# One diffusion-transformer step on one core: q and gate tiles evicted by ScalarE, a modulation piece's rows multiplied in reverse, the first rotary copy emitted earlier

## The chip, the cores and the metric

The kernel runs on one core of one Trainium2 chip. A core has TensorE (PE in the profile, with its weight loads as PEld), VectorE (DVE), ScalarE (ACT), GpSimd (POOL) and SyncE (SP), whose queue issues nearly all DMAs here. Each engine runs its instructions in the order of its own queue; semaphores join the queues. The metric is the device time of one execution in microseconds (us), as the median of several runs.

## What is computed

The reference is one step of a two-layer diffusion trunk on 640 tokens (128 context, 512 latent) with 2048 channels, all in float32. Cut to what matters here:

```python
m = silu(cond) @ w_mod + b_mod                 # modulation: shift, scale, gate (6144 columns), for two conditions
h = rmsnorm(x, g) * (1 + scale) + shift
# layer 0: latent attention (A, 8 heads) beside a bidirectional recurrence (B, "HGRN", 8 heads)
q_lat, kv_lat, k_pe, a_gate, b_q, b_ff, b_fb, b_i, b_gate = split_cols(h @ w_in, AB_SIZES)
q = rmsnorm(rmsnorm(q_lat, ..) @ w_q_up, ..)   # the last 64 of 192 channels of a head get a rotary embedding
o_a = blocked_attention(q, keys, vals) * silu(a_gate)
qb = silu(b_q);  o_b = hgrn_bidir(qb, b_i, b_ff, b_fb, ..)
o_b = rmsnorm(o_b) * silu(b_gate)
x = x + gate * (concat([o_a, o_b]) @ w_out)
# layer 1: windowed grouped-query attention, with its own modulation, input and output projection
```

## The kernel before

The tokens lie on the free axis: a tile of 128 channels is 128x640, and a matmul's result holds 128x320 of it, so each tile of a projection is two halves (HALF = 320) in two PSUM banks of the tag `acc`. There are two such banks in the stages below, so the first half of a tile must be evicted before the next tile may begin.

Products of full precision are made of three matmuls on float32 values split in a high and a low part (`three`, L113 to L115): high weight by high activation, high by low, low by high. The third (L115) is the one that needs the low part of the weights. `unit` brings 512 KB of weights (the DMA at L100, into one of four `raw` buffers), and `split` makes the two parts: L75 on ScalarE copies the high part, L76 on VectorE subtracts. `coltile` runs one tile of the projection from the normalised input: two units, each 48 matmuls (8 blocks by three, for each of the two halves).

The stages, with their times in the profile before: start, modulation and first part of the input projection (0 to 245 us); the eight HGRN heads (245 to 980), about 92 us each; the gates of attention heads 2 to 7 and what the latent attention sets up (980 to 1050); the latent (MLA) attention heads, into which the first half of the output projection is woven (`out_b`, to about 1370); the other half; the second layer (from 1500).

**An HGRN head** (`hgrn_head`) runs coltile for the two forget gates, for q, for v (`vr`) and, later, for its output gate. `evict_silu` (L496 on) takes q and the output gate out of PSUM: two VectorE operations of 128x320 (L501, a copy bounded below by XMIN), a sigmoid of three ScalarE operations (`sigmoid`, L70 to L72), one product. `attn_gate` uses it for the attention's gates too (tile `lat`). Beside this stand the recurrence's scans (L539, L540) and its pieces on VectorE, ScalarE (L554, L603) and TensorE (L578, L604).

**Modulation beside the heads.** `pump`, called once a unit, takes the next piece of one of two streams. One is `mod_sums`, on VectorE: loads at L310, sums at L317, four small matmuls at L323. The other is `mod_blocks`, on TensorE: pieces of two weight rows, each row a 512 KB load (L290) into a `raw` buffer and four matmuls of 128x256 (L292) that are summed in the bank `m` over all 16 rows. The `raw` buffers are shared by `unit`, both streams and `head_prep`.

**The start of the MLA heads** (in `run`). Eight finished mix tiles are loaded (`xb`, L1239, two buffers) and split into `act` by L75 and L76. `rope_queries(0)` computes the rotary queries `qr` of a pair of heads, `head_prep(0)` the keys and queries of head 0 (L816 to L818, L825 to L827) and its norms, which pass through small DMAs (L89, L91, L837, L839). `rope_split` makes `qrh` of `qr`: two ScalarE copies of 64x640 (L876), a DMA of each to the other half of the partitions (L877), two memsets, and two VectorE subtractions for the low part (L881). The scores of head 0 need it first at L900.

**What sets the order.** The source's order gives each instruction a priority, `ahead()` raises it for what is inside, and the framework's scheduler then lays out each engine's queue from priorities, dependencies and its own estimate of durations. So an edit in one place can shift instructions elsewhere. Line numbers after the change are 5 higher from L291 on and 6 higher behind `evict_silu`.

Of the kernel before, what the change touches and what calls it, by code (L numbers as in the profile page):

```python
# [10 lines left out]
AF = mybir.ActivationFunctionType  # L11
ALU = mybir.AluOpType
AX = mybir.AxisListType

P = 128
D = 2048
KT = 16
# [3 lines left out]
HALF = T // 2  # L21
EPS = 1e-6
BIG = -1e30
XMIN = -43.0
# [4 lines left out]
class Trunk:  # L29
# [252 lines left out]
    def mod_blocks(self, l, bs, pool):  # L282

        nc = self.nc
        wm = self.io[f"mod_w_{l}"][0].rearrange("(k p) c -> p k c", p=P)
        for b in bs:
            ps = self.w("m")[:, :256]
            for k in range(KT):
                raw = self.t(self.rawp, [P, 1024], tag="raw")
                nc.sync.dma_start(raw, wm[:, k, 1024 * b:1024 * b + 1024])  # L290
                for g in range(4):  # L291
                    nc.tensor.matmul(ps[32 * g:32 * g + 32, :], lhsT=self.sc[:, k, :], rhs=raw[:, 256 * g:256 * g + 256],  # L292
                                     start=k == 0, stop=k == KT - 1)
                if k % 2 and k < KT - 1:
                    yield
            row = self.t(pool, [P, 256], tag="mrow")
            nc.scalar.activation(row, ps, AF.Copy)
            for c in range(2):
                nc.sync.dma_start(self.mrow[l][c, 4 * b:4 * b + 4], row[c:P:32])
            yield  # L300
# [194 lines left out]
    def evict_silu(self, pool, pts, tag):  # L495

        nc = self.nc
        x = self.t(pool, [P, T], tag=tag, bufs=2 if tag == "q" else 1)
        s = self.t(self.gatep, [P, T], tag="sil")
        for i, p in enumerate(pts):  # L500
            nc.vector.tensor_scalar(x[:, HALF * i:HALF * i + HALF], p, scalar1=XMIN, scalar2=None, op0=ALU.max)  # L501
        self.sigmoid(s, x)
        nc.vector.tensor_tensor(x, x, s, op=ALU.mult)
        return x
# [692 lines left out]
    def run(self):  # L1197
        nc, tc, io = self.nc, self.tc, self.io
        self.setup()
        pool = lambda name, side="right", bufs=1: tc.tile_pool(name=name, bufs=bufs, side=side, reuse_waits="tile")  # L1200
        for n, rows in (("gates", D // 2), ("xT", D), ("xb", D), ("x1", D), ("mixc", D), ("lat", 7 * P)):
            setattr(self, n, self.t(self.dram, [rows, T], tag=n))
        self.mix = [self.t(self.dram, [P, T], tag=f"mix{k}") for k in range(KT)]
        self.mrow = {l: self.t(self.dram, [2, 24, 256], tag=f"mrow_{l}") for l in ("ab", "c")}
        with self.banked(acc=2, m=2, w=4), pool("start") as sp:
            with pool("xin", "left") as xin:
                self.conditioning(xin)
                self.read_x(xin, sp)
                self.parameters(xin)
            late = ExitStack()  # L1210
            self.act[1] = late.enter_context(pool("act1", "left", 8))
            self.start()
        with late:
            self.gatep = late.enter_context(pool("gatep", "left"))
            with self.banked(acc=2, w=3, o=2, m=1):
                with pool("bp") as bp:
                    self.hgrn_setup(bp)
                    self.units = 0
                    onpe = chain(self.mod_blocks("ab", range(4, 6), bp), self.mod_blocks("c", range(2), bp))
                    ondve = self.mod_sums("c", range(4, 8), bp)  # L1220
                    self.stream = (onpe, ondve, onpe, ondve, iter(()))
                    for h in range(HEADS):
                        mix = self.hgrn_head(h, bp)
                        nc.sync.dma_start(self.mix[8 + h], mix)
                    assert all(next(x, self) is self for x in self.stream)
                    self.stream = None
                    self.mod_columns("ab", 32, 48, bp, "fin0")
                    self.mod_columns("c", 0, 32, bp, "fin1")
                apool = pool("ap")
                ap = apool.__enter__()  # L1230
                with pool("ap0") as ap0:
                    self.mla_setup(ap, ap0)
                for h in range(self.early, HEADS):
                    self.attn_gate(h)
        with pool("pair") as pair, pool("aleft", "left") as left, self.banked(acc=2, w=5, o=1):
            act = [None] * KT
            for k in range(8, 16):
                x = self.t(left, [P, T], tag="xb", bufs=2)
                nc.sync.dma_start(x, self.mix[k])  # L1239
                act[k] = self.t(self.act[0], [P, 2, T + 2], F32R, tag="act")[:, :, 0:T]  # L1240
                self.split(act[k][:, 0], act[k][:, 1], x)
            self.mla_pools(ap, pair, left)
            with self.ahead():
                for _ in chain(self.rope_queries(0), self.head_prep(0)):
                    pass
            self.out_b(0, act, left)
            f = 1
            for h in range(HEADS):
                if h % 2 == 0:
                    self.rope_split()  # L1250
                side = iter(())
                if h + 1 < HEADS:
                    side = chain(self.rope_queries(h // 2 + 1) if h % 2 else (), self.head_prep(h + 1))
                for _ in self.head_attention(h):
                    with self.ahead():
                        next(side, None)
                for _ in side:
                    pass
                for _ in range((1, 1, 2, 2, 2, 2, 2, 3)[h]):
                    self.out_b(f, act, left)  # L1260
                    f += 1
        apool.__exit__(None, None, None)
        with (pool("gatep", "left") as self.gatep, pool("act1c", "left", 8) as self.act[1],
              self.banked(acc=3, w=4, o=1)):
            self.R = self.t(self.gatep, [P, T], tag="R")
            with pool("am") as am, pool("oab") as sp:
                for k in range(8):
                    x = self.t(am, [P, T], tag="mixin", bufs=3)
                    nc.sync.dma_start(x, self.mix[k])
                    act[k] = self.t(am, [P, 2, T], F32R, tag="mixa", bufs=8)  # L1270
                    self.split(act[k][:, 0], act[k][:, 1], x)
                self.out_ab(act, sp)
            with pool("op") as op:
                with pool("cp") as cp:
                    self.tabC = self.t(cp, [P, 2, TS], tag="tabC")
                    nc.sync.dma_start(self.tabC, io["k_ropeC"])
                    self.band = self.t(cp, [P, 7 * P], tag="band")
                    nc.sync.dma_start(self.band, io["k_band"])
                    self.units = 0
                    self.stream = (self.mod_sums("c", range(8, 12), cp),)  # L1280
                    for g in range(4):
                        outs = self.gqa_group(g, cp, op)
                    assert next(self.stream[0], self) is self
                    self.stream = None
                    self.mod_columns("c", 32, 48, cp, "kout")
                self.out_c(outs, op)
# [75 lines left out]
```

## Time and profile before

| | |
|---|---|
| median of 3 runs | 2435.55 us (2435.2 to 2436.18) |
| the profiled execution | 2439.68 us, its span 2437.7 us |
| granted TensorE clock, mean | 0.994 |
| TensorE busy | 2398.5 us, 98% of the span |
| VectorE busy | 1439.2 us, 59% |
| ScalarE busy | 914.6 us, 38% |
| TensorE idle, whole span | 39.2 us |
| of it in 245 to 980 / 1050 to 1100 | 8.7 us / 5.8 us |

All instants in this text are us from the start of the span. A line of a timeline names the start, the duration, the engine, the line of the source, the operation and its output and inputs; in brackets stands how long the engine was idle just before and which instruction ended that. A line of the waits names the waiting engine and instruction, what it waited for, the total, the number of times and the longest. The granted clock is the share of TensorE's full clock that the chip gave in that stretch.

### The profile page before, as it was taken

The numbers are of one execution on the slowest core, as the hardware profiler recorded it, in microseconds if no ns is written. First come the engines' busy times: TensorE is split into PE (matmuls) and PEld (weight loads), VectorE is DVE, ScalarE is ACT, GpSimd is POOL, SyncE is SP. The second block draws the span as 40 slices with busy tenths as digits, with TensorE's granted clock in tenths as the row PEclk, the third lists the DMA queues.
The fourth block names the chain that finished last, engine by engine and source line by source line (L and its number), as shares of the span: only waits on it lengthen the run. The fifth ranks groups of instructions, "written<-read, shape, count | busy, mean of one in ns | idle before, by whom it ended". The sixth has DMA issues, their size and how long they took to land.

```text
span 2437.7 us, 42188 instructions
## 1 busy us (share of the span) xinstructions
PE 2398.5 (98%) x17230; PEld 2290.4 (94%) x17230; DVE 1439.2 (59%) x2985; ACT 914.6 (38%) x1719; POOL 59.4 (2%) x81
## 2 busy tenths in 40 slices
PE   7999999999999999999999999999999999999999
PEld 4789999999999999989999999999999999999999
DVE  5556666666666666555555668778755554554221
ACT  4323333333333333454445432343353443453211
POOL 1000000000000000000000120000000000000000
PEclk8999999999999999999999999999999999999999
DMA  9974534434444433443433655435522222225332
GB/s 309 307 255 149 158 115 141 141 115 146 139 117 144 132 116 111 146 139 106 131 113 115 206 168 160 124 102 158 145 72 75 76 81 78 73 66 165 113 113 61
DMA packets 402177, 328.12 MB, mean 135 GB/s; under 512 B 36410, under 2 KB 348160, under 8 KB 401472
## 3 DMA queue, kind: packets, MB, share of 16 engines
q1 hardware_dynamic: 401408, 325.34, 44.5%
q8 instruction: 135, 2.21, 0.4%
q0 software_dynamic: 576, 0.09, 0.1%
q14 instruction: 58, 0.48, 0.1%
HBM read 280.73 MB, written 36.79 MB: 130 GB/s over the span
## 4 chain that ended last, share of the span: by engine, by line
PE 89%; DMA 6%; DVE 3%; ACT 1%; issue 1%; SPq 0%; ACTq 0%; DVEq 0%
PE acc L113 23%; PE acc L115 22%; PE acc L114 22%; PE w L48 3%; DMA raw<-in_mod_w_ab_dram 2%; PE w L113 2%; PE o L1178 2%; PE w L114 2%; PE w L115 2%; DMA raw<-in_mod_w_c_dram 2%; PE w L604 2%; PE o L924 1%; PE m L269 1%; PE m L292 1%; DVE split L76 1%
## 5 line engine op out<-in xcount | busy, mean ns | idle before, releaser
L113 PE MATMUL acc<-act,split 128*128 128x320 f32 (+1 forms) x3552 | 1116.4, 315 | 13.1 <-DVE q L501 8.7
L114 PE MATMUL acc<-act,split 128*128 128x320 f32 (+1 forms) x3552 | 1111.9, 313 | 0.8 <-DVE act L76 0.8
L115 PE MATMUL acc<-act,split 128*128 128x320 f32 (+1 forms) x3552 | 1110.5, 313 | 0.6 <-DVE split L76 0.6
L113 PEld LDWEIGHTS acc<-act,split 128*128 128x128 f32 x3552 | 671.3, 189 | 52.7 <-issue 17.0
L115 PEld LDWEIGHTS acc<-act,split 128*128 128x128 f32 x3552 | 669.4, 189 | 6.3 <-issue 2.7
L114 PEld LDWEIGHTS acc<-act,split 128*128 128x128 f32 x3552 | 670.0, 189 | 5.0 <-DVE act L76 2.0
L75 ACT ACTIVATE split<-raw 128x1024 fp32r<-128x1024 f32 (+4 forms) x297 | 285.4, 961 | 649.9 <-PE acc L115 564.0
L76 DVE TENSOR_TENSOR split<-raw,split 128x1024 fp32r<-128x1024 f32 (+4 forms) x297 | 326.7, 1100 | 215.7 <-ACT split L75 214.2
L317 DVE SCALAR_TENSOR_TENSOR macc<-raw,sc,macc 128x512 f32<-128x512 f32 x240 | 171.0, 748 | 62.1 <-DMA raw<-in_mod_w_c_dram 62.0
L114 PE MATMUL acc<-mc,split 128*128 128x320 f32 x256 | 80.3, 314 | 0.0
L113 PE MATMUL acc<-mc,split 128*128 128x320 f32 x256 | 79.1, 314 | 0.0
L115 PE MATMUL acc<-mc,split 128*128 128x320 f32 x256 | 79.0, 309 | 0.0
L113 PE MATMUL acc<-mixa,split 128*128 128x320 f32 x256 | 78.8, 308 | 0.0
L114 PE MATMUL acc<-mixa,split 128*128 128x320 f32 x256 | 78.8, 308 | 0.0
L115 PE MATMUL acc<-mixa,split 128*128 128x320 f32 x256 | 78.7, 308 | 0.0
L576 DVE COPY_PREDICATED PS<-masks,w 128x384 f32<-128x384 uint8 x80 | 38.6, 516 | 61.2 <-PE w L604 42.0
L1161 ACT ACTIVATE sc<-sc,mxc,rqc 128x512 f32<-128x512 f32 (+2 forms) x80 | 55.9, 699 | 40.4 <-DVE mxc L1160 40.3
L1156 DVE CUSTOM_DVE_ANT_0 sc<-w,band 128x512 f32<-128x512 f32 (+2 forms) x80 | 43.4, 555 | 45.4 <-PE w L115 45.2
L412 DVE TENSOR_TENSOR lat<-lat,acc 128x320 f32<-128x320 f32 (+1 forms) x72 | 34.9, 485 | 59.4 <-PE acc L115 59.1
L1175 ACT ACTIVATE pTc<-w 128x512 f32<-128x512 f32 (+2 forms) x80 | 37.8, 485 | 66.3 <-PE w L48 65.1
L953 DVE SCALAR_TENSOR_TENSOR y<-acc,mod_c,y 128x320 f32<-128x320 f32 (+2 forms) x48 | 19.5, 437 | 72.6 <-PE acc L115 72.6
L1178 PE MATMUL o<-pTc,vc 128*128 128x128 f32 x448 | 58.2, 275 | 0.0
(395 smaller groups left out, 3265.0 us busy)
## 6 DMA issues: line engine op xcount, KB each, us to landing
raw<-in_mod_w_ab_dram SPq DMA_DIRECT2D x96, 512.0 KB
raw<-in_mod_w_c_dram SPq DMA_DIRECT2D x96, 512.0 KB
raw<-in_w_in_ab_dram SPq DMA_DIRECT2D x92, 512.0 KB
raw<-in_w_in_c_dram SPq DMA_DIRECT2D x80, 512.0 KB
raw<-in_w_out_ab_dram SPq DMA_DIRECT2D x32, 512.0 KB
raw<-in_w_out_c_dram SPq DMA_DIRECT2D x32, 512.0 KB
raw<-in_w_in_ab_dram SPq DMA_DIRECT2D x24, 256.0 KB
xT<-xT SPq DMA_DIRECT2D x4, 1280.0 KB
```

The source lines that it names most:

```text
L48: self.nc.tensor.transpose(out, in_, self.ident[:k, :k])
L75: self.nc.scalar.activation(hi, full, AF.Copy)
L76: self.nc.vector.tensor_tensor(lo, full, hi.bitcast(F32), op=ALU.subtract)
L113: mm(out, lhsT=w[0], rhs=a[0], start=start, stop=False)
L114: mm(out, lhsT=w[0], rhs=a[1], start=False, stop=False)
L115: self.last = mm(out, lhsT=w[1], rhs=a[0], start=False, stop=stop).ins
L317: nc.vector.scalar_tensor_tensor(acc[:, c], raw[:, i], s, acc[:, c], op0=ALU.mult, op1=ALU.add)
L576: nc.vector.copy_predicated(dst[:, c0:c1], self.masks[:, mi].unsqueeze(1).to_broadcast([P, c1 - c0, P]), p[:, :P * (c1 - c0)].rearrange("p ...
L604: select(PS, 2 + li, lambda o, c: nc.tensor.matmul(o.rearrange("p (n d m) -> p n d m", d=2, m=m), lhsT=km[:, P * c:P * c + P], rhs=pairs(Q ...
L1156: nc.vector.tensor_tensor_reduce(s, in0=p, in1=self.band[:, m0:m0 + n], scale=1.0, scalar=-3e38, op0=ALU.add, op1=ALU.max, accum_out=mx[:, ...
L1161: nc.scalar.activation(s, s, AF.Exp, bias=mx[:, 2:3], scale=rq[:, b:b + 1], accum_out=mx[:, 0:1])
L1178: nc.tensor.matmul(od, lhsT=v[:, k0 // P + c], rhs=pT[:, c], start=c == 0, stop=c == nb - 1)
```

## The change

Three edits. `evict_silu` takes each half out of PSUM by a ScalarE copy (L506) and then bounds the whole tile on SBUF by one VectorE operation (L507). `mod_blocks` issues the loads of a piece's two rows first and then multiplies the second row before the first; the sum starts with row 1 and stops with row 14. `run` calls the first `rope_split` inside `ahead()`, between `rope_queries(0)` and `head_prep(0)`; the loop calls it only for heads 2, 4 and 6.

```diff
--- before.py
+++ after.py
@@ mod_blocks
-            for k in range(KT):
-                raw = self.t(self.rawp, [P, 1024], tag="raw")
-                nc.sync.dma_start(raw, wm[:, k, 1024 * b:1024 * b + 1024])
-                for g in range(4):
-                    nc.tensor.matmul(ps[32 * g:32 * g + 32, :], lhsT=self.sc[:, k, :], rhs=raw[:, 256 * g:256 * g + 256],
-                                     start=k == 0, stop=k == KT - 1)
-                if k % 2 and k < KT - 1:
+            for k0 in range(0, KT, 2):
+                raws = []
+                for k in (k0, k0 + 1):
+                    raw = self.t(self.rawp, [P, 1024], tag="raw")
+                    nc.sync.dma_start(raw, wm[:, k, 1024 * b:1024 * b + 1024])
+                    raws.append((k, raw))
+
+                for k, raw in raws[::-1]:
+                    for g in range(4):
+                        nc.tensor.matmul(ps[32 * g:32 * g + 32, :], lhsT=self.sc[:, k, :],
+                                         rhs=raw[:, 256 * g:256 * g + 256], start=k == 1, stop=k == KT - 2)
+                if k0 < KT - 2:
                     yield
@@ evict_silu
         for i, p in enumerate(pts):
-            nc.vector.tensor_scalar(x[:, HALF * i:HALF * i + HALF], p, scalar1=XMIN, scalar2=None, op0=ALU.max)
+            nc.scalar.activation(x[:, HALF * i:HALF * i + HALF], p, AF.Copy)
+        nc.vector.tensor_scalar(x, x, scalar1=XMIN, scalar2=None, op0=ALU.max)
         self.sigmoid(s, x)
@@ run
             with self.ahead():
-                for _ in chain(self.rope_queries(0), self.head_prep(0)):
+                for _ in self.rope_queries(0):
+                    pass
+                self.rope_split()
+                for _ in self.head_prep(0):
                     pass
...
-                if h % 2 == 0:
+                if h % 2 == 0 and h > 0:
                     self.rope_split()
```

The queues move at three places. The first is VectorE and ScalarE at the q tile of HGRN head 3 (`q` is the tile, `acc` its banks, `split_5407` and `split_5414` the first weights of the tile that follows). VectorE before:

```order
L539 SCALAR_TENSOR_TENSOR L_5485<-reset_2427,lf_5486 128x640
L540 SCALAR_TENSOR_TENSOR L_5485<-reset_2427,lf_5486 128x640
L76 TENSOR_TENSOR split_5407<-raw_5405,split_5407 128x1024
L56 SCALAR_TENSOR_TENSOR osq_4944<-w_4947,osq_4944 128x256
L501 TENSOR_SCALAR q_5329<-acc_5203 128x320
```

ScalarE after the change, at the same place:

```order
L75 ACTIVATE split_5414<-raw_5412 128x1024
L506 ACTIVATE q_5335<-acc_5209 128x320
L560 ACTIVATE TT_5504<-L_5492 128x160
L75 ACTIVATE split_5659<-raw_5657 128x1024
L506 ACTIVATE q_5335<-acc_5210 128x320
```

On VectorE the first half stood behind the scans and the low half of the next weights; on ScalarE it stands directly behind their high half, and the second half behind L560 (a read of the scan's result) and one more split.

The second is TensorE in the piece of modulation that runs beside head 3's output gate (`raw_5025` and `raw_5031` before are row 0 and row 1, `raw_5031` and `raw_5033` after). Before:

```order
L292 MATMUL m_4187<-raw_5025,sc_124 32x256 x4
L292 MATMUL m_4187<-raw_5031,sc_124 32x256
L604 MATMUL w_4704<-lf_4640,km_4702 128x128 x3
L604 MATMUL w_4709<-lf_4640,km_4702 128x128 x2
L292 MATMUL m_4187<-raw_5031,sc_124 32x256 x2
```

After the change:

```order
L297 MATMUL m_4191<-raw_5033,sc_124 32x256 x4
L297 MATMUL m_4191<-raw_5031,sc_124 32x256
L610 MATMUL w_4709<-lf_4645,km_4707 128x128 x3
L610 MATMUL w_4714<-lf_4645,km_4707 128x128 x2
L113 MATMUL acc_4966<-act_476,split_4969 128x320
```

The rows of the piece change places, and the two matmuls that followed L604 have gone to join the last one further on.

The third is SP and ScalarE at the start of the MLA heads. SP before:

```order
L89 DMA sums_10172<-sumrow_10170 4x160
L91 DMA sums_10174<-sums_10172 128x5x1
L100 DMA raw_10967<-in_w_out_ab_dram 128x8x128
L1239 DMA xb_10014<-mix_27_104 128x640
L877 DMA qrh_10258<-qrh_10258 64x640 x2
L1239 DMA xb_10019<-mix_28_105 128x640
```

SP after:

```order
L89 DMA sums_10203<-sumrow_10201 4x160
L100 DMA raw_10989<-in_w_out_ab_dram 128x8x128
L91 DMA sums_10205<-sums_10203 128x5x1
L1245 DMA xb_10036<-mix_27_104 128x640
L1245 DMA xb_10041<-mix_28_105 128x640
L883 DMA qrh_10112<-qrh_10112 64x640 x2
```

ScalarE before:

```order
L75 ACTIVATE act_10006<-xb_10004 128x640
L54 ACTIVATE kr_10153<-kr_10153 128x192
L816 ACTIVATE ksq_10289<-w_10290 128x384
L817 ACTIVATE kh_10288<-w_10290,cols_143_500 128x384
L876 ACTIVATE qrh_10258<-qr_10050 64x640 x2
L75 ACTIVATE act_10011<-xb_10009 128x640
```

ScalarE after:

```order
L75 ACTIVATE act_10028<-xb_10026 128x640
L54 ACTIVATE kr_10184<-kr_10184 128x192
L75 ACTIVATE act_10033<-xb_10031 128x640
L822 ACTIVATE ksq_10311<-w_10322 128x384
L823 ACTIVATE kh_10310<-w_10322,cols_143_500 128x384
L882 ACTIVATE qrh_10112<-qr_10072 64x640 x2
```

The rope copies stand behind one more split than before, their DMAs behind one more xb load, and the load of the output weights ahead of L91. On TensorE the second block of 12 latent-query matmuls of head 1 (L113 to L115 on `qlh`), which stood behind L900 and L901 of head 0, now stands ahead of them.

## The prediction

> **What bounds the kernel now.** I read the page's busy times first, then a table of the span by stage, then what TensorE waits for. The page (busy us, share of the span, instructions):
>
> ```profile
> PE 2398.5 (98%) x17230; PEld 2290.4 (94%) x17230; DVE 1439.2 (59%) x2985; ACT 914.6 (38%) x1719; POOL 59.4 (2%) x81
> ```
>
> TensorE is busy 98% of the span, so anything that another engine gains counts only where TensorE stands idle: 39.2 us in all. The windows give the two stages that the change touches (stretch, its length, busy time of each engine, granted TensorE clock, DMA share, GB/s):
>
> ```profile
> 245.00:980.00 735.00, 726.28 (x5311) 687.28 (x5310) 479.74 (x735) 248.12 (x338) 8.87 (x14) 1.00 0.44 131
> ...
> 1050.00:1100.00 50.00, 44.21 (x315) 41.74 (x314) 32.97 (x82) 30.41 (x63) 0.00 (x0) 0.93 0.55 156
> ```
>
> The eight HGRN heads (245 to 980) leave TensorE 8.7 us idle, the start of the MLA heads (1050 to 1100) 5.8 us, there with a clock below 1. TensorE's waits (total us, times, longest) name the causes:
>
> ```profile
> PE acc L113 <- DVE q L501: 8.7, 6, 1.8
> ...
> PE w L900 <- DMA qrh<-qrh: 3.4, 1, 3.4
> PE acc L113 <- ACT act L75: 2.2, 2, 1.6
> ...
> PE acc L114 <- DVE act L76: 0.8, 2, 0.6
> ```
>
> All 8.7 us of the heads are one wait: the tile after q cannot start until VectorE has evicted q's first half. In the MLA start it is the copy of the rope queries by DMA.
>
> **Eviction by ScalarE: the work itself.** Prices (x count, busy us, mean ns):
>
> ```profile
> L501 DVE TENSOR_SCALAR q<-acc 128x320 f32<-128x320 f32 x16 | 7.8, 485 | 0.0
> ```
>
> ```profile
> L518 ACT ACTIVATE vr<-acc 128x320 f32<-128x320 f32 x16 | 6.9, 430 | 19.3 <-PE acc L115 19.3
> ```
>
> ```profile
> L911 DVE TENSOR_SCALAR s<-s,mx 128x640 f32<-128x640 f32 x32 | 17.6, 551 | 0.6
> ```
>
> 44 half tiles (16 of q, 16 of gate, 12 of lat) leave VectorE at 0.485 us, 22 whole-tile bounds come at 0.551: 21.3 - 12.1 = 9.2 us less there. ScalarE gets 44 x 0.430 = 18.9 us more. Neither engine is the bound (33% and 65% busy in the heads), so by itself this is worth nothing. The SiLU's chain starts about 1 us later behind the first half's arrival. What covers it: in head 3 q is evicted at 548 to 550, and the first matmul that needs its product comes 17 us later:
>
> ```profile
> 567.61 0.83 PE L578 MATMUL w<-lf,e 128*128 128x128 f32 x6
> ```
>
> TensorE's list has no wait for that product.
>
> **Eviction by ScalarE: the stalls.** What counts is when TensorE may start the tile after q. For each of the six heads with a stall, here are VectorE's L76 (the low half of that tile's first weight split, which stands in its queue just ahead of L501) and TensorE's restart (start us, duration, the idle time before):
>
> ```profile
> 269.67 1.20 DVE L76 TENSOR_TENSOR split<-raw,split 128x1024 fp32r<-128x1024 f32 x1
> ...
> 454.31 1.20 DVE L76 TENSOR_TENSOR split<-raw,split 128x1024 fp32r<-128x1024 f32 x1
> ...
> 546.66 1.20 DVE L76 TENSOR_TENSOR split<-raw,split 128x1024 fp32r<-128x1024 f32 x1
> ...
> 638.52 1.20 DVE L76 TENSOR_TENSOR split<-raw,split 128x1024 fp32r<-128x1024 f32 x1
> ...
> 822.66 1.21 DVE L76 TENSOR_TENSOR split<-raw,split 128x1024 fp32r<-128x1024 f32 x1
> ...
> 917.35 1.20 DVE L76 TENSOR_TENSOR split<-raw,split 128x1024 fp32r<-128x1024 f32 x1
> ```
>
> ```profile
> 272.70 0.41 PE L113 MATMUL acc<-act,split 128*128 128x320 f32 x1 [1.83 <-DVE q L501]
> ...
> 456.30 0.41 PE L113 MATMUL acc<-act,split 128*128 128x320 f32 x1 [1.35 <-DVE q L501]
> ...
> 547.05 0.61 PE L323 MATMUL w<-macc,ones 128*32 128x256 f32 x8
> 548.65 0.41 PE L113 MATMUL acc<-act,split 128*128 128x320 f32 x1 [0.99 <-DVE q L501]
> ...
> 640.50 0.41 PE L113 MATMUL acc<-act,split 128*128 128x320 f32 x1 [0.93 <-DVE q L501]
> ...
> 824.65 0.42 PE L113 MATMUL acc<-act,split 128*128 128x320 f32 x1 [1.83 <-DVE q L501]
> ...
> 916.93 0.61 PE L323 MATMUL w<-macc,ones 128*32 128x256 f32 x8
> 919.33 0.41 PE L113 MATMUL acc<-act,split 128*128 128x320 f32 x1 [1.79 <-DVE q L501]
> ```
>
> ScalarE is idle then, so the copy is done when TensorE has finished q. But the stall does not simply vanish, because L76 is late next: the third matmul (L115) reads its result. The chain of waits shows how the third follows a stalled first one:
>
> ```profile
> 549.21 0.15 PE acc L115
> ```
>
> That is 0.56 us behind the stalled start, and 0.30 (two matmuls) behind an unstalled one. So per head the third matmul moves from "restart + 0.56" to the later of "TensorE free + 0.30" and "L76 done + 0.04". Head 0: free at 270.87, L76 done at 270.87, so from 273.26 to 271.17: 2.1. Head 2: 456.86 to 455.55: 1.3. Head 4: 641.06 to 639.87: 1.2. Head 6: 825.21 to 823.91: 1.3. In heads 3 and 7 the eight L323 matmuls now fill 0.61 us ahead of the stall; in the new order they come about 50 matmuls later, so that filling is lost: 549.21 to 547.90 and 919.89 to 918.59, 1.3 less 0.6, 0.7 each. Sum 7.3 us. Bounds: 10.3 if L76 moved up too (8.7 and six times 0.26 of restart), 2 if whatever is next on VectorE gives most of it back. I take 7.3, since every term has its own row.
>
> The second half of q now stands on ScalarE behind L560, which waits for a scan, and behind a weight split. By the same rows it ends near 549.1 in head 3, and TensorE wants that bank 24 matmuls (3.5 us) after 547.6, at 551.1: 2.0 us of cover, so nothing. The evictions of gate and lat have at most one split (1.06 us) and their own copy (0.43) before them, also less than those 3.5 us: nothing.
>
> **Reversed rows of a modulation piece.** The same 256 matmuls and 64 loads. Two prices are possible: the group now begins with the load that is issued second, and another buffer comes free first. Head 3 (TensorE's L292, records x10 and x2 of one piece; SP's issues; one load of such a row in the chain; the split that a later load feeds):
>
> ```profile
> 585.91 1.05 PE L292 MATMUL m<-raw,sc 128*32 128x256 f32 x10
> ...
> 592.49 0.62 PE L292 MATMUL m<-raw,sc 128*32 128x256 f32 x2
> ```
>
> ```profile
> 566.50 1.20 SPq L290 DMA_DIRECT2D raw<-in_mod_w_c_dram  x2
> ...
> 586.61 1.01 SPq L100 DMA_DIRECT2D raw<-in_w_in_ab_dram  x2
> ```
>
> ```profile
> 532.98 6.29 DMA raw<-in_mod_w_c_dram
> ```
>
> ```profile
> 592.59 1.06 ACT L75 ACTIVATE split<-raw 128x1024 fp32r<-128x1024 f32 x1 [3.54 <-PE acc L115]
> ```
>
> The two loads were issued by 567.7 and, at 6.29 us for one, had landed by 574, 12 us before use. And the buffer that comes free at 585.91 is still the one for the load at 586.61: it is only the other of the two rows. The mod matmuls moved within the piece (5 and 3 instead of 5, 2 and 1) fill no stall. Zero, with bounds of a few tenths either way.
>
> **The first rope copy.** In the queues it comes no sooner. On ScalarE the two copies now stand behind the second activation split, on SP their DMAs behind the fourth xb load; the w_out load moves up, and TensorE gets 12 latent-query matmuls ahead of L900. SP's issues, ScalarE's copies, the chain and two windows:
>
> ```profile
> 1060.62 0.53 SPq L89 DMA_DIRECT2D sums<-sumrow  x1
> ...
> 1064.02 0.48 SPq L100 DMA_DIRECT2D raw<-in_w_out_ab_dram  x1
> ```
>
> ```profile
> 1064.35 1.50 ACT L876 ACTIVATE qrh<-qr 64x640 fp32r<-64x640 f32 x2
> ```
>
> ```profile
> 1065.36 6.87 DMA qrh<-qrh
> 1072.27 0.47 PE w L900
> ...
> 1077.06 0.28 PE w L115
> ```
>
> ```profile
> 1068.00:1072.20 4.20, 0.86 (x4) 0.60 (x4) 1.38 (x5) 0.99 (x3) 0.00 (x0) 0.88 0.76 186
> ...
> 1076.00:1078.00 2.00, 2.00 (x9) 2.00 (x9) 0.00 (x0) 0.64 (x2) 0.00 (x0) 0.50 0.64 168
> ```
>
> The copies start some 0.6 us later, so the DMA is issued near 1066.0. In front of it, 512 KB of w_out, 320 of xb and its own 320 took from 1064.02 to 1072.2: 140 KB/us. Now w_out is issued right behind L89, near 1061.2, and is through; two xb and qrh, 960 KB from about 1064.6 at 140 to 180 KB/us, end at 1069.9 to 1071.5. I take 1070.7; the far bound is 1066.0 + 6.87 = 1072.9. TensorE ran out at 1072.27 - 3.4 = 1068.9; with the 0.8 us of waits for act gone and 12 matmuls (1.8 us) more it runs out at 1069.9, or 1068.9 if small gaps close too: 1069.4, so it idles 1.3 us instead of 3.4. After the 3.4 us the clock was 0.50 (last window) for nearly 6 us; after the heads' 1.83 us it stayed at 1.00. So I expect no slow stretch: these 18 matmuls end at 1070.7 + 0.9 = 1071.6 instead of 1077.3, 5.7 us sooner. Not all of that is kept. The seventh and eighth activation splits (the 1.6 us wait for L75) come through two xb buffers, and their loads are paced by DMA: at worst they move only by w_out's 2.8 us, at best by 5.7. I take 4.0 for the whole place, with bounds 1 (late landing, slow clock again) and 5.7.
>
> The Trainium skill, "TensorE: Matmul & The Clock Gate", Part 1 (The HAM clock gate), has the clock fall to half after one idle window of about 3.4 us and come back after as long a busy time. By that rule a gap of 1.3 us costs no clock and one near 3.4 us may, which this trace bears out on both sides; what it would cost here is a rival below.
>
> **Sum.** 7.3 + 0 + 4.0 = 11.3 us. The profiled execution took 2439.68 us (span 2437.7), 4.1 more than the median of the three runs, 2435.55; I take the same gain off both: 2428.4 for a profiled run, 2424.3 for the median. A measurement of this kernel can tell about 0.2%, 4.9 us.
>
> **Rivals.**
> 1. *The gain in the heads is given back* (chance 0.15). VectorE carries 65% in the heads and its chain of loads, scans and masks does not get shorter; if its next result is late by what TensorE gained, 1.5 us of the 7.3 stay, with 1 at the rope copy: 2435.55 - 2.5 = 2433.0, no difference. For it: L76 is already the next one late in four heads. Against: no other wait in the heads is on record.
> 2. *The rope copy lands late and the clock falls* (0.15). Landing at 1072.9, TensorE idles 3.5 us and runs at half clock afterwards; of 4.0 only 1 is left: 2435.55 - 8.3 = 2427.3. By the clock rule cited above it is the free-running window that decides.
> 3. *Both chains are freer than I think* (0.08): 10.3 + 5.7 = 16, 2419.6.
> 4. *Slower: the freed buffer* (0.07). If the load at 586.61 had to wait for the row that is now multiplied last, it would be issued at 593.2 and land at 599.5, so that the split of 592.59 starts 6.9 us late. With its 2.3 us for both halves, against the 7.2 us (48 matmuls) of the weights already split, TensorE would stall 2.0 us a head, and some 3 with the gate eviction queued behind that split on ScalarE: 8 x 3.0 - 11.3 = +12.7, 2448.3. From 2.0 us a head it ends slower. Against it stands the order of the buffers above.
>
> The forecast itself has 0.55. Faster by over 0.2%: 0.55 + 0.15 + 0.08, 0.78, less 0.02 for forecasts that fall short: 0.76. Same: 0.15 + 0.02 = 0.17. Slower: 0.07. The range reaches from 2419.7, the freest case, to 2433.5, just past the first rival.
>
> **What would show it.** Right: the wait for q L501 gone, in its place waits of L115 for split L76 of about 3 us in all; ScalarE's eviction at 0.43 us; the wait of L906 for qrh at 1 to 2 us and no window at 0.50; SP's weight loads at the same places between TensorE's matmuls. Wrong: a wait for the second half of q on ScalarE, SP loads that move behind the last L297 of a piece, the clock at 0.50 again, or a wait for act L75 grown by more than 3 us.

## The result and the profile after

The changed kernel takes 2421.6 us (median of 4 runs, 2418.55 to 2425.33) where the kernel before takes 2435.6 (4 runs beside them): 14.0 us less, a ratio of 0.9946 (95% interval 0.9933 to 0.9958, or 10 to 16 us less). The forecast was 2424.3, a gain of 11.3. The sum came out near; three of its four parts did not. The page after, and two windows that answer to those of before:

```profile
PE 2390.7 (99%) x17230; PEld 2284.1 (94%) x17230; DVE 1430.2 (59%) x2963; ACT 930.0 (38%) x1763; POOL 59.4 (2%) x81
```

```profile
245.00:980.00 735.00, 734.69 (x5404) 697.66 (x5404) 478.37 (x726) 265.85 (x380) 8.88 (x14) 1.00 0.45 133
...
1050.00:1100.00 50.00, 44.13 (x325) 42.46 (x324) 31.68 (x85) 26.98 (x56) 0.00 (x0) 0.97 0.57 158
```

In the heads TensorE's idle time fell from 8.7 to 0.3 us. But its busy time over the whole span fell too, by 7.8 us for the same 17230 instructions: part of the gain lay in time that counted as busy. TensorE's waits after:

```profile
PE acc L113 <- ACT act L75: 4.9, 3, 2.4
...
PE w L906 <- ACT act L75: 1.6, 1, 1.6
...
PE acc L115 <- DVE split L76: 0.4, 1, 0.4
...
PE acc L113 <- ACT q L506: 0.3, 1, 0.3
```

The wait for q's eviction is gone; nothing took its place (the one wait for `split L76` is at 1640 us and stood in the trace of before as well). The wait of the first rope scores halved, and a wait for the activation splits grew.

Where the time went is read best between two instructions that both kernels have: the first eviction of a forget gate and the first of v in head 7 (ScalarE, before and after).

```profile
239.73 0.42 ACT L514 ACTIVATE e<-acc 128x320 f32<-128x320 f32 x1
...
930.19 0.44 ACT L518 ACTIVATE vr<-acc 128x320 f32<-128x320 f32 x1 [2.45 <-PE acc L115]
```

```profile
241.33 0.42 ACT L520 ACTIVATE e<-acc 128x320 f32<-128x320 f32 x1
...
917.99 0.44 ACT L524 ACTIVATE vr<-acc 128x320 f32<-128x320 f32 x1 [0.17 <-PE acc L115]
```

690.46 against 676.66 us: 13.8 less in the heads, where 7.3 was forecast. The second stretch, called the MLA stretch below, reaches from the query sums of MLA head 0 (`sqq`) to the first values product of its first latent block (`o`), again before and after:

```profile
1059.26 0.58 PE L84 MATMUL w<-sqq,ones 128*32 128x160 f32 x6
...
1093.95 0.83 PE L924 MATMUL o<-pT,vA 128*128 128x128 f32 x6
```

```profile
1047.16 0.58 PE L84 MATMUL w<-sqq,ones 128*32 128x160 f32 x6
...
1080.41 0.83 PE L930 MATMUL o<-pT,vA 128*128 128x128 f32 x6
```

It took 34.69 before and 33.25 after: 1.4 less, where 4.0 was forecast. The loads at the start happened to cost the second run 1.6 more, and the rest of the program gave 0.6.

### The profile page after: what moved, and what is told of

Same layout as the page of the kernel before. It is cut to its first block, busy times and chain, and to the rows that moved or that the text cites. A ratio compares the mean times of both kernels' runs of the same rounds, so it can differ in the third digit from the quotient of the medians.

```text
span 2423.5 us, 42208 instructions
## 1 busy us (share of the span) xinstructions
PE 2390.7 (99%) x17230; PEld 2284.1 (94%) x17230; DVE 1430.2 (59%) x2963; ACT 930.0 (38%) x1763; POOL 59.4 (2%) x81
## 4 chain that ended last, share of the span: by engine, by line
PE 92%; DMA 4%; DVE 2%; ACT 1%; issue 0%; SPq 0%; ACTq 0%; DVEq 0%
PE acc L113 24%; PE acc L115 24%; PE acc L114 23%; PE w L48 3%; PE o L1184 2%; PE w L113 2%; PE w L114 2%; PE w L115 2%; PE w L610 2%; PE o L930 1%; PE m L297 1%; PE m L269 1%; DMA raw<-in_mod_w_ab_dram 1%; DMA xb<-mix 1%; DMA raw<-in_w_in_ab_dram 1%; PE w L641 1%
## 5 line engine op out<-in xcount | busy, mean ns | idle before, releaser
L113 PE MATMUL acc<-act,split 128*128 128x320 f32 (+1 forms) x3552 | 1116.3, 315 | 7.6 <-ACT act L75 4.9
L115 PE MATMUL acc<-act,split 128*128 128x320 f32 (+1 forms) x3552 | 1110.1, 313 | 0.4 <-DVE split L76 0.4
L113 PEld LDWEIGHTS acc<-act,split 128*128 128x128 f32 x3552 | 670.3, 189 | 46.8 <-issue 22.2
L115 PEld LDWEIGHTS acc<-act,split 128*128 128x128 f32 x3552 | 668.5, 188 | 6.1 <-issue 2.4
L75 ACT ACTIVATE split<-raw 128x1024 fp32r<-128x1024 f32 (+4 forms) x297 | 285.2, 960 | 618.2 <-PE acc L115 523.2
L76 DVE TENSOR_TENSOR split<-raw,split 128x1024 fp32r<-128x1024 f32 (+4 forms) x297 | 326.4, 1099 | 212.8 <-ACT split L75 205.4
L113 PE MATMUL acc<-mc,split 128*128 128x320 f32 x256 | 79.1, 314 | 0.0
L115 PE MATMUL acc<-mc,split 128*128 128x320 f32 x256 | 79.0, 309 | 0.0
L115 PE MATMUL acc<-mixa,split 128*128 128x320 f32 x256 | 78.8, 308 | 0.0
L113 PE MATMUL acc<-mixa,split 128*128 128x320 f32 x256 | 78.8, 308 | 0.0
L1162 DVE CUSTOM_DVE_ANT_0 sc<-w,band 128x512 f32<-128x512 f32 (+2 forms) x80 | 43.4, 554 | 45.6 <-PE w L115 45.5
```

Source lines behind the costliest of these rows:

```text
L75: self.nc.scalar.activation(hi, full, AF.Copy)
L76: self.nc.vector.tensor_tensor(lo, full, hi.bitcast(F32), op=ALU.subtract)
L113: mm(out, lhsT=w[0], rhs=a[0], start=start, stop=False)
L115: self.last = mm(out, lhsT=w[1], rhs=a[0], start=False, stop=stop).ins
L1162: nc.vector.tensor_tensor_reduce(s, in0=p, in1=self.band[:, m0:m0 + n], scale=1.0, scalar=-3e38, op0=ALU.add, op1=ALU.max, accum_out=mx[:, ...
```

## The experiments

Every kernel was run beside the kernel before on the same chip, whose median was 2433.3 to 2435.0 us there. The queues of each, laid beside those of the two kernels, show one thing: the reversed rows alone, and the earlier rope copy alone, leave every queue of TensorE, ScalarE and SP in the order of before, but for which of a piece's two rows comes first; and the eviction edit alone gives all the movements of the changed kernel. So the new order at the start of the MLA heads, which the prediction put down to the rope edit, comes from the eviction of `lat`.

A group, or visit, is in what follows a run of modulation matmuls (L292, L297 or L298) that stand next to each other in TensorE's queue. The 32 pieces of eight matmuls stand in 54 groups in the kernel before and in 47 in the changed one, where 17 pieces are in one group each, 8 in two of four, and 7 in one of five and one of three (before: five, two and one).

**The eviction alone** (`evict_only`): the changed kernel without the edits in `mod_blocks` and `run`.

> Only the eviction edit; the modulation rows and the rope copy as before. Theory A (all movement of the queues comes from the eviction edit, the other two edits change neither the queues nor the time): as the changed kernel, 2421.6 us within its scatter of 3 us, with the same six stalls gone in the HGRN heads and the same order at the start of the MLA heads. Theory B (the prediction: the rope edit brings the rope copy's 4.0 us): 2435.6 - 7.3 = 2428.3 us, with the rope copy as before, a wait of 3.4 us and a slow clock behind it.

Measured: 2423.1 us (2420.7 to 2424.6), ratio 0.9950 (0.9932 to 0.9969). The heads took 676.8 us. Theory A: it carries the whole change.

**The reversal alone** (`reverse_only`): the kernel before with the hunk in `mod_blocks` only.

> Only the reversed rows of the modulation pieces. Theory A: 2435.6 us, no difference, the groups of modulation matmuls as before (5, 2 and 1). Theory B (the changed kernel's pieces, 5 and 3 matmuls instead of 5, 2 and 1, come from the reversal and save a switch of the array each): eight switches of some 0.3 us, 2433.2 us.

Measured: 2435.2 us, ratio 1.000 (0.999 to 1.001), with 54 groups. Zero, as the prediction had it.

**The rope copy alone** (`rope_only`): the kernel before with the hunks in `run` only.

> The kernel before with only the first rope_split emitted earlier. Theory A (it changes no queue: every engine's rows stand as before): no difference, 2434 us within the scatter of the kernel before, qrh's DMA again between the third and the fourth xb load. Theory B (the prediction's 4.0 us belong to this edit): 2430 us.

Measured: 2431.9 us, ratio 0.9991 (0.9980 to 1.0001). No difference that can be told from none. The 4.0 us of Theory B would be 0.9984, which is inside the interval, so time alone does not exclude it; that no queue moved does. Its trace has the wait for qrh again, though only 1.8 us of it:

```profile
PE w L900 <- DMA qrh<-qrh: 1.8, 1, 1.8
```

**Only q by ScalarE** (`q_only`): the changed kernel with

```diff
-            nc.scalar.activation(x[:, HALF * i:HALF * i + HALF], p, AF.Copy)
-        nc.vector.tensor_scalar(x, x, scalar1=XMIN, scalar2=None, op0=ALU.max)
+            if tag == "q":
+                nc.scalar.activation(x[:, HALF * i:HALF * i + HALF], p, AF.Copy)
+            else:
+                nc.vector.tensor_scalar(x[:, HALF * i:HALF * i + HALF], p, scalar1=XMIN, scalar2=None, op0=ALU.max)
+        if tag == "q":
+            nc.vector.tensor_scalar(x, x, scalar1=XMIN, scalar2=None, op0=ALU.max)
```

> The changed kernel with gate and lat evicted by VectorE again, q by ScalarE. Theory A: the stalls (8.7 and six restarts of 0.26) go and with them the half clock behind head 6's stall (1.5), the rest as before: 2435.6 - 11.8 = 2423.8 us; the start of the MLA heads as before, with the 3.4 us wait for qrh and a clock of 0.50 after it. Theory B (the low half of the next weights is late next and keeps 3 us of the stalls): 2435.6 - 7.3 = 2428.3 us, with waits of L115 for L76 in six heads.

Measured: 2429.5 us (2425.6 to 2432.2), ratio 0.9976 (0.9966 to 0.9986): 5.5 us. The gain is smaller than either theory's (11.8 and 7.3), but the mechanism is A's: of the stalls this is left,

```profile
PE acc L113 <- ACT q L507: 0.2, 1, 0.2
```

and no wait of L115 for a weight split in the heads. What was too large is the stall that I took off. The recorded profile of before was a bad one of its kind: the four traces with its queues in the heads had 690.46 (that one), 686.69 (`reverse_only`), 686.57 (`lat_only`) and 685.26 us (`rope_only`) in the heads, 687.2 in the mean, with 8.7, 4.8, 4.9 and 5.2 us of waits for q. `q_only` has 681.6: 5.6 below that mean, and 8.9 below the recorded profile.

**Only the first half by ScalarE** (`first_half`):

```diff
+            if i == 0:
+                nc.scalar.activation(x[:, HALF * i:HALF * i + HALF], p, AF.Copy)
+            else:
+                nc.vector.tensor_scalar(x[:, HALF * i:HALF * i + HALF], p, scalar1=XMIN, scalar2=None, op0=ALU.max)
+        nc.vector.tensor_scalar(x[:, :HALF], x[:, :HALF], scalar1=XMIN, scalar2=None, op0=ALU.max)
```

> The changed kernel, but ScalarE takes only the first half of each tile out of PSUM; the second half is evicted and bounded by VectorE as before. Theory A (only the first half's eviction is waited for; the new grouping of the modulation matmuls needs both halves): stalls at q gone as in q_only, 54 groups, start of the MLA heads as before: 2429.5 us. Theory B (the second half is late next on VectorE): waits for DVE q of 1 us and more per head, 2432 us or over.

Measured: 2428.7 us, ratio 0.9981 (0.9969 to 0.9992). As `q_only`, with 54 groups and the old order in the MLA heads; one wait for q of 1.3 us was left. The first half is what TensorE waits for.

**All but lat by ScalarE** (`lat_by_vector`): the diff of `q_only` with `tag != "lat"` for `tag == "q"`.

> The changed kernel with lat alone evicted by VectorE again, q and gate by ScalarE. Theory A (the gate's edit joins the modulation matmuls to 5 and 3, 8 times 0.3 us; lat's edit both reorders the start of the MLA heads and delays the last gate's SiLU by 1.8 us, so that the first xb loads come 2 us late): q 11.8 and groups 2.4 off, 2421.4 us, the first act wait of 2.4 us gone, the wait for qrh back to 3.4. Theory B (lat's eviction by ScalarE is a plain gain at the start of the MLA heads): slower than the changed kernel by 2 us or more, 2423.6 us and over.

Measured: 2424.0 us (2422.8 to 2426.6), ratio 0.9959 (0.9943 to 0.9975). The heads took 677.2 us, 4.4 less than with q alone, and in each of the seven heads from the second on it is 0.71 or 0.72 less (5.0 together; the first head lost 0.6). The MLA stretch took 36.5 us, the longest of all traces. The interval of the ratio overlaps that of `evict_only`, so the time does not say what lat is worth.

**Only the output gates** (`gate_only`): the kernel before, its eviction by ScalarE for `tag == "gate"`.

> The kernel before with only the eight output gates evicted by ScalarE. Theory A (the edit makes the scheduler join the last two visits of modulation matmuls of each gate tile, which saves 0.71 us a head in seven heads, as between q_only and lat_by_vector): 2435.0 - 5.0 = 2430.0 us, the stalls at q as before. Theory B (the gate's gain needs q's: an unstalled head first shows it): 2435 us, no difference.

Measured: 2428.4 us, ratio 0.9982 (0.9972 to 0.9991): 4.9 us, with 47 groups. Theory A. The stalls at q stayed (6.7 us in its list of waits), so this gain is its own.

**Only the attention gates** (`lat_only`): the same for `tag == "lat"`.

> The kernel before with only the six late attention gates (lat) evicted by ScalarE. Theory A: this edit alone brings the new order at the start of the MLA heads (12 matmuls ahead of the first rope scores, the output weights' load ahead of L91), and the last gate's SiLU starts 1.8 us later, so that the first xb loads come some 2 us late: the wait for act L75 of about 2 us appears, the stretch from head 0's key sums to the first rope scores grows by 1.6, the one behind it shrinks by 3: 2433.6 us. Theory B (the late SiLU costs nothing, the new order gives the 4.0 us of the prediction): 2431.0 us.

Measured: 2432.8 us, ratio 1.0000 (0.9992 to 1.0009). The gain of Theory B, 4.0 us, would be 0.9984 and lies outside the interval; that of Theory A, 1.4, would be 0.9994 and cannot be told from zero. The queue at the start of the MLA heads is the changed kernel's, the waits for `act L75` are 4.1 us (2.0 to 3.6 in the traces with the old order), and the MLA stretch took 30.75 us.

The gate's gain had no wait to its name, so I looked at TensorE's own row. Here is the place in head 3 where the queues differ, before and after:

```profile
585.91 1.05 PE L292 MATMUL m<-raw,sc 128*32 128x256 f32 x10
586.89 1.38 PE L604 MATMUL w<-lf,km 128*128 128x128 f32 x10
588.21 0.62 PE L292 MATMUL m<-raw,sc 128*32 128x256 f32 x4
588.76 0.42 PE L113 MATMUL acc<-act,split 128*128 128x320 f32 x1
```

```profile
582.24 1.05 PE L297 MATMUL m<-raw,sc 128*32 128x256 f32 x10
583.22 1.38 PE L610 MATMUL w<-lf,km 128*128 128x128 f32 x10
584.36 0.39 PE L113 MATMUL acc<-act,split 128*128 128x320 f32 x1
```

From the start of the masked products (L604, L610) to the projection's next matmul it is 1.87 us with the visit of two modulation matmuls and 1.14 without: 0.73. Those two join the last visit of the piece, of one matmul before and of three after, and cost nearly nothing there: 0.54 us from its start to the projection's next matmul before, 0.57 after.

```profile
592.49 0.62 PE L292 MATMUL m<-raw,sc 128*32 128x256 f32 x2
593.03 0.41 PE L113 MATMUL acc<-act,split 128*128 128x320 f32 x1
```

```profile
588.05 0.63 PE L297 MATMUL m<-raw,sc 128*32 128x256 f32 x6
588.62 0.41 PE L113 MATMUL acc<-act,split 128*128 128x320 f32 x1
```

(The trace has two records for each of these matmuls, so x2 is one of them.) If a visit costs some 0.7 us, more and fewer visits must show it. Two kernels raise the priority of a piece's eight matmuls in the changed kernel:

```diff
-                for k, raw in raws[::-1]:
-                    for g in range(4):
+                with self.tc.high_priority(offset=400):
+                  for k, raw in raws[::-1]:
+                    for g in range(4):
```

With 400 the scheduler puts all 32 pieces in one group each; with 20 it scatters them (204 groups instead of 47).

> The changed kernel with a slightly raised priority for the same matmuls, by which the scheduler scatters them: 204 visits, 189 of them a single matmul between two of the projection. Theory A (0.35 us or more a visit): 157 visits more, 55 to 110 us, 2477 to 2531 us. Theory B (visits cost nothing): 2422 us within 4.

Measured: 2530.2 us, ratio 1.0402 (1.0388 to 1.0416). Against the changed kernel's 2421.6 that is 108.6 us for 157 visits, 0.69 us each, with no new wait in the list. TensorE counts it as busy: 2499.9 us of its time against 2390.7. (The two ran on different chips; by their ratios it is 0.71 a visit.) In the heads (245 to 980) the modulation matmuls of the kernel before, of the changed one and of the scattered one (which reaches fewer of them in that window) read:

```profile
L292 PE MATMUL m<-raw,sc 128*32 128x256 f32 x496 | 43.4, 388 | 0.0
```

```profile
L297 PE MATMUL m<-raw,sc 128*32 128x256 f32 x496 | 39.1, 388 | 0.0
```

```profile
L298 PE MATMUL m<-raw,sc 128*32 128x256 f32 x448 | 111.5, 391 | 0.0
```

The mean of one is nearly the same in all; the busy time grows because in a group the matmuls overlap each other and alone they do less. Laid end to end, 496 records of 388 ns would take 192 us; in the groups of the changed kernel they take 39.1. The 448 of the scattered one would take 175 and take 111.5.

> The changed kernel with the eight modulation matmuls of a piece at a raised priority, so that all 32 pieces stand in one group (32 visits instead of 47). Theory A (each visit among the projection's matmuls costs TensorE 0.35 to 0.7 us): 15 visits less, 5 to 10 us, 2412 to 2417 us, if the loads have landed. Theory B (the visits cost nothing, gate's 0.71 us a head has another cause): 2421.6 us, or slower where a whole group now waits for its second row.

Measured: 2419.5 us (2418.6 to 2421.6), ratio 0.9948 (0.9935 to 0.9960): against the changed kernel's 0.9946, on another chip, no gain to be seen. TensorE had five waits for a modulation row, together 4.0 us, which the changed kernel doesn't have:

```profile
PE m L298 <- DMA raw<-in_mod_w_ab_dram: 2.4, 3, 1.9
...
PE m L298 <- DMA raw<-in_mod_w_c_dram: 1.6, 2, 0.8
```

So both were run side by side (`changed_again` and `joined400_again`, the same two kernels).

> The changed kernel on the same chip as the next one: 2421.6 us within 3.

> The changed kernel with joined pieces, beside the changed kernel on the same chip. Theory A: 3 us faster than it, by the checkpoints of the first run (heads 1.9, attention gates 1.3, of a possible 7 with 4 us of new waits for the second row). Theory B: no difference beyond 1 us.

Measured: 2421.3 us (2419.8 to 2423.6, ratio 0.9946, 0.9932 to 0.9959) and 2416.2 us (2414.0 to 2419.6, ratio 0.9925, 0.9911 to 0.9939). Joining the rest is worth 5.2 us here, 0.35 a visit: half the price of a visit. Waits for rows take 1.4 us in this trace. Most of the remainder can be read from the starts in the changed kernel. A visit of four:

```profile
569.80 0.64 PE L297 MATMUL m<-raw,sc 128*32 128x256 f32 x8
570.37 0.41 PE L113 MATMUL acc<-act,split 128*128 128x320 f32 x1
```

From its start to the next matmul that follows it is 0.57 us, as with a visit of three; with one of five it is 0.98 and with one of eight 1.00. So up to four matmuls cost about the same, and four more add 0.43. Joining a five and a three saves 0.55, about as joining the two and the one did; joining two fours saves 0.14. With some 0.17 for leaving the projection and coming back (the 0.71 a head less 0.54), 7 visits of the first kind and 8 of the second give an estimate of 7.5 us, and 6.1 with the waits off. This version beats both kernels.

## Why the prediction was right in its sum and wrong in its parts

**The stalls at q: 7.3 forecast, 5.5 measured, and by another way.** The step "L76 is late next: the third matmul (L115) reads its result" failed. I took the split that stands ahead of L501 on VectorE for the first weights of the next tile (the description of the change says so too). It is the second unit's: the queue shows the v tile's first matmul reading another split, and the one in question only 48 matmuls later.

```
L113 MATMUL acc_5338<-act_476,split_5342 128x320      (first matmul of v in head 3, before)
L113 MATMUL acc_5338<-act_1358,split_5407 128x320     (where split_5407 is first read)
```

So nothing holds TensorE at that place. Head 7 after the change shows it: TensorE goes from modulation into v with no wait, and its third matmul starts at 906.75, before L76 has even begun.

```profile
906.99 1.20 DVE L76 TENSOR_TENSOR split<-raw,split 128x1024 fp32r<-128x1024 f32 x1
```

```profile
905.35 1.07 PE L297 MATMUL m<-raw,sc 128*32 128x256 f32 x16
906.35 0.41 PE L113 MATMUL acc<-act,split 128*128 128x320 f32 x1
906.61 0.31 PE L114 MATMUL acc<-act,split 128*128 128x320 f32 x1
906.75 0.31 PE L115 MATMUL acc<-act,split 128*128 128x320 f32 x1
```

A second misreading went the same way: "after the heads' 1.83 us it stayed at 1.00". The window of 735 us rounded it away. Behind head 6's stall the clock did fall:

```profile
815.00:822.00 7.00, 7.00 (x53) 6.72 (x54) 6.70 (x9) 0.88 (x1) 0.00 (x0) 1.00 0.15 36
...
825.60:828.80 3.20, 3.20 (x14) 3.20 (x14) 3.20 (x7) 2.31 (x4) 0.00 (x0) 0.50 1.01 352
```

That is 3.2 us at half speed, 1.6 lost, behind a gap well short of 3.4, so this trace does not bear the clock rule out on both sides, as the prediction had it. The stalls whole with their restarts (10.3) and this, less L323's filling in two heads (1.2), make 10.7 for the recorded trace; against it `q_only` has 8.9, since head 0 kept 0.7, heads 2, 4 and 6 gained 0.2 to 0.3 less than their stalls, and the two heads without a stall lost 0.3 each. On the other side the stalls of the recorded profile were nearly twice those of three other traces of the same queues, so against the median less was to be had. The errors went opposite ways: 7.3 was sized on the wrong mechanism and the wrong base, and missed 5.5 by 1.8.

**The evictions themselves** bring no wait of their own, as said, apart from `lat` below: ScalarE's copy takes 0.42 to 0.44 us in the rows, VectorE's bound 0.48 to 0.49 (0.55 forecast).

**The modulation pieces: 0 forecast, 4.9 measured.** "The mod matmuls moved within the piece (5 and 3 instead of 5, 2 and 1) fill no stall. Zero" asked only what they hide, not what it costs TensorE to turn to them and back: 0.7 us a visit, seven visits. And this is the gate edit's doing (`gate_only`), not the reversal's. The reversal's own zero was right.

**The rope copy: 4.0 forecast, none from that edit; the stretch itself gained 1.4.** The order moved as described, but by the eviction of lat. The step that failed in the stretch is "the evictions of gate and lat ... nothing". At the last attention gate, VectorE's copy before ran beside ScalarE's split of the next weights, and the SiLU could start at 1050.82, 1.2 us after TensorE had left the tile (at 1049.66):

```profile
1049.86 1.06 ACT L75 ACTIVATE split<-raw 128x1024 fp32r<-128x1024 f32 x1 [6.18 <-PE acc L115]
1050.82 0.72 ACT L70 ACTIVATE sil<-lat 128x640 f32<-128x640 f32 x1
```

After, the copy waits behind that split on ScalarE, and the bound behind its low half on VectorE:

```profile
1037.77 1.06 ACT L75 ACTIVATE split<-raw 128x1024 fp32r<-128x1024 f32 x1 [3.08 <-PE acc L115]
1038.73 0.42 ACT L506 ACTIVATE lat<-acc 128x320 f32<-128x320 f32 x1
1040.52 0.74 ACT L70 ACTIVATE sil<-lat 128x640 f32<-128x640 f32 x1 [1.37 <-DVE lat L507]
```

```profile
1038.86 1.23 DVE L76 TENSOR_TENSOR split<-raw,split 128x1024 fp32r<-128x1024 f32 x1 [6.28 <-ACT split L75]
1040.00 0.49 DVE L507 TENSOR_SCALAR lat<-lat 128x640 f32<-128x640 f32 x1
```

That is 3.0 us after TensorE's leaving (1037.57): 1.8 later. I asked only when TensorE needs the bank, not what else stands behind the SiLU on ScalarE: head 0's weight split, its queries, and by them the issues on SP. That chain is read from the queues and was not tried by itself; that the eviction of `lat` brings the delay is shown, for in all seven traces where ScalarE evicts the whole of `lat` the first xb load is issued 1.0 to 1.3 us behind the query sums, and in the other seven 0.6 to 0.8 ahead of them. Here the first xb loads, 8.8 us behind TensorE's leaving before, are 10.8 behind it after:

```profile
1058.42 0.89 SPq L1239 DMA_DIRECT2D xb<-mix  x2
```

```profile
1048.40 0.88 SPq L1245 DMA_DIRECT2D xb<-mix  x2
```

TensorE then waits 2.4 us for the first activation split, and 1.6 for the rope scores:

```profile
1054.06 0.55 PE L113 MATMUL acc<-act,split 128*128 128x320 f32 x2 [2.41 <-ACT act L75]
1061.22 0.30 PE L906 MATMUL w<-kr,qrh 128*128 128x128 f32 x1 [1.61 <-ACT act L75]
```

The second is near the 1.3 forecast, though it names a split: the copies stand behind the splits, and all of it had become later together. In the other trace of the changed kernel (`changed_again`) it is 1.6 us as well and names qrh's DMA, the sign that the prediction gave. The 3.4 us before, from which it was reckoned, was the longest of the seven traces with the old order (1.2 to 3.4). The clock did fall once after the change, behind the wait of 1.85 us at 1072. The 0.94 over 13.6 us is 1.6 us at half speed, so with the 1.7 of the second line it lasted 3.3 us, from about 1073.1 on:

```profile
1061.20:1074.80 13.60, 11.73 (x96) 10.62 (x97) 9.74 (x26) 8.50 (x18) 0.00 (x0) 0.94 0.65 186
1074.80:1076.50 1.70, 1.70 (x8) 1.70 (x8) 0.32 (x1) 0.77 (x3) 0.00 (x0) 0.50 0.76 199
```

So the slow stretch that the prediction saw vanish comes and goes in both orders: in 1050 to 1100 (1150 to 1200 in `joined20`) the granted clock was 0.90 to 1.00 in the traces with the old order and 0.93 to 1.00 in those with the new one, 1.00 in `changed_again`.

Over the traces, the MLA stretch took 33.5 us in the mean of seven with the old order (31.2 to 36.5) and 31.4 in the mean of seven with the new one (30.2 to 33.3): a gain of 2.1 that the scatter nearly hides, and `lat_only` could not show in the time. From the first rope scores (L900) on, the two orders hardly meet, 19.2 to 24.4 us against 16.4 to 19.2, but 1.8 us of that are the 12 matmuls that now stand ahead of the scores.

**Rivals.** The first (the gain in the heads is given back) and the fourth (the freed buffer) did not occur: TensorE waits for no load in the heads after the change, where SP's weight loads moved only ahead of small stores, and the reversal alone took 2435.2. Of the second, the clock's fall came in one of the two traces of the changed kernel, but without the 3.5 us of idle time. The third, both chains freer at 2419.6, came nearest in size, but through visits it did not know of.

**The sum.** By single edits: q 5.5, gate 4.9, lat 0 to 2.1, rope and reversal 0: 10.4 to 12.5, beside 11.9 for the evictions together and 12.7 to 14.0 for the whole. The intervals reach 2 to 5 us to either side, so these agree; what remains open is the last 2 us, and how much of lat's order is gain. That the forecast came near was luck: the 4.9 us of the visits, which it had at nothing, stood in for what the stalls at q and the rope copy fell short.

## What to carry to other kernels

Ask of every small matmul that a scheduler tucks between large ones what turning to it costs, not only what it hides: the price stands in no list of waits, but in the busy time of its group (43.4 us against 39.1 for the same 496 records). Before costing an eviction, follow the names: which split, which bank, and what stands behind the evicting instruction on its own engine. And size a stall from several traces, since it may be half as long in the next one. See which edit moves a queue by laying each edit's queues beside those of before.

## What was not expected of the hardware

One visit of TensorE to a single 32-column matmul among 128-column ones cost 0.69 us in the mean of 157 more such visits; a visit of two cost 0.73 at the one place read out. A visit of one matmul delays the projection's next one by nearly as much as a visit of four (0.54 against 0.57 us from start to start), and one of eight by 1.00.

The granted clock fell to 0.50 behind waits of some 1.8 us, not only behind the one of 3.4: behind head 6's 1.83 us before, for at least 3.2 us, and behind 1.85 us at the MLA start after, for 3.3; yet not behind head 0's 1.83, nor behind the 1.61 before the rope scores, nor behind the 2.41 before the first activation split. So the length of one wait does not decide it alone. The Trainium skill ("TensorE: Matmul & The Clock Gate", Part 1: The HAM clock gate) asks for an idle window of about 3.4 us; these traces show the fall after less idle time than that.
